# Four more low parts of two pooling groups by adding transfers, and each pooling group's newest columns ahead of later low parts on GpSimd

## The chip, the cores and the metric

One core of one Trainium2 chip runs the whole kernel in one launch. The metric is the device time of an execution in microseconds (us); the time before is the median of three runs.

## The reference

One layer of a hybrid decoder on 256 prompt columns and 8 x 4 sample columns, T = 288 columns in all, with 2048 channels, in float32:

```
h = rmsnorm(x, norm1_g)
proj = h @ w_in + b_in                       # 3072 columns: a, gate, z
u = a * sigmoid(gate)                        # 1024 channels
c = silu(layernorm(depthwise_causal_conv(concat(history, u), conv_w, conv_b)))   # 31 taps
d = multiscale_pool(concat(history, z))      # 4 groups, windows 2, 4, 8, 16
p = (d per group @ pool_w) * pool_scale
x = x + concat(c, p) @ w_out
x = x + square(relu(rmsnorm(x, norm2_g) @ w_ff1)) @ w_ff2
y = rmsnorm(x, norm_f)
```

The new convolution and pooling states are outputs too.

## The kernel before, in words

Channels lie on the 128 partitions and the 288 columns along the free side, so each matrix product is a sum of 128x128 weight tiles times 128x288 activations. Every product is done in three passes on rounded numbers: an activation or weight is split in a high part (`hi`, rounded to fp32r) and a low part (`lo` = raw - hi), and the sum takes hi x hi, lo x hi and hi x lo. Two k-tiles of one output tile make a group of six matmuls in `gemm`: two with weights `whi`, two with `wlo`, two with `whi`.

Weights come from `io["w"]` in blocks of 2048 or 1024 rows x 256 columns; a half of such a block (4 k-tiles, 512 KB) is loaded in one transfer by SP into a raw tile `wr` (6 buffers) and split into `whi` and `wlo` (5 buffers each). PE uses such a half part for 24 matmuls. The number behind a name (wlo14) counts the half parts in the order of use: wlo1 to wlo8 belong to the first two convolution pairs, wlo9 to wlo12 to `c2`, 13 to 16 to `c3`, 17 to 20 to `c4`, 21 to 24 to pooling group `p3`, 25 to 28 to `c5`, 29 to 32 to `p2`, 33 to the small product `P3`, 34 to 37 to `c6`, 38 to 41 to `p1`, 42 to `P2`, 43 to 46 to `p0`, 47 to `P1`, 48 to 51 to `c7`, 52 to `P0`, and from 53 on to the output projection (`w0`, `w1`, ...), then to the MLP.

`split_part` makes the high part on ACT always (line L260). The low part is made in one of three ways, chosen by the letter in the table `WAYS` for the stage and the place in it:
- `V`: one subtraction on DVE (L265);
- `G`: two subtractions of half the tile on GpSimd, called POOL in the profile (L268);
- `D`: ACT writes -hi into `lo` (L262) and a transfer issued by POOL adds the raw weights from memory onto it (L263).

The stages stand in `SEQUENCE`: c0 c1 c2 c3 c4 p3 c5 p2 P3 c6 p1 P2 p0 P1 c7 P0. A `c` stage (`conv_products`, `conv_pair`) makes two output tiles, the gated `u`, and then the convolution: the taps of the prompt columns on DVE (L448), those of the sample columns as one product `prd` on POOL (L451) and a sum on DVE. A `p` stage (`pool_group`) makes two tiles of `z`, running sums `s` by doubling on POOL (L479), and from them the pooled differences `d`: prompt columns on DVE (L484), the newest (sample) columns on POOL (L486, L487). A `P` stage (`pool_products`) multiplies `d` with the pooling weights. `gemm` takes its `between` as work put into its order ahead of a given k.

The order on each engine comes from a scheduler that places instructions by priority as the program is written, along a simulated timeline; `tc.issue_after(x)` puts an instruction behind x. On PE the order is held by a chain. Convolution taps are written under `later()`, with lower priority. The order of the matmuls inside a product can be altered: `classes` is a string that asks for matmuls of class 0 or 1 (parity of k plus the choice of the activation's part) in turn, and `TURN` is such a string, of 48 places, used in `c2`, `c5`, at the start of the output projection and in a few products after it. Everywhere else the six matmuls of a group follow each other as above. Product results go to two PSUM buffers `ac`, so a product must wait until the last but one is read.

Of the kernel before, what the change touches and what calls it, by code (L numbers as in the profile page):

```python
# [12 lines left out]
ALU = mybir.AluOpType  # L13
# [56 lines left out]
TURN = "110100" * 4 + "01" * 6 + "1100" * 3  # L70


WAYS = {"c2": "GVGV", "c3": "GDGG", "c4": "GDGD", "p3": "GDDG", "c5": "GDGD", "c": "GGGV", "p": "GVVG", "w0": "VV", "w": "GG", "ff": "VV"}


VEC = (("norm1_g", 16), ("b_in", 24), ("conv_b", 8), ("ln_g", 8), ("ln_b", 8), ("pool_scale", 8), ("norm2_g", 16), ("norm_f", 16))
# [10 lines left out]
def trunk_kernel(ctx: ExitStack, tc: tile.TileContext, io):  # L87
# [46 lines left out]
    def f32(t):  # L134
        return t.bitcast(F32)
# [25 lines left out]

    blocks = iter(range(5, io["w"].shape[0]))

    def load():

        src, raw = io["w"][next(blocks)], []
        for h in range(2):
            raw.append((raw_tile(), src[:, 4 * h : 4 * h + 4, :]))
            nc.sync.dma_start(*raw[-1])
        return raw  # L170
# [78 lines left out]
        last = mm(psum[:, 0, :T], minus, total, start=True, stop=True)  # L249
        return row_of(psum, psum[:, 0, :T], *args), last  # L250

    turns = {}

    def split_part(raw, src, hi, lo, way):

        nc.scalar.copy(hi, raw)  # L260
        if way == "D":
            nc.scalar.activation(lo, f32(hi), AF.Copy, scale=-1.0)  # L262
            nc.gpsimd.dma_start(lo, src, accum_op=ALU.add)  # L263
        elif way == "V":
            nc.vector.tensor_tensor(lo, raw, f32(hi), op=ALU.subtract)  # L265
        else:
            for j in range(0, raw.shape[1], 2):
                nc.gpsimd.tensor_tensor(lo[:, j : j + 2, :], raw[:, j : j + 2, :], f32(hi[:, j : j + 2, :]), op=ALU.subtract)  # L268

    def spl():  # L270
        return [wspl.tile([P, 4, 256], F32R, name=nm("w" + part), tag="w" + part) for part in ("hi", "lo")]
# [21 lines left out]
            chain[0] = last.ins  # L293
        return last

    def gemm(banks, rhs, m_outer=False, between={}, classes="", by_part=False, gets=None, pairs=None):


        n = len(rhs)
        gets = gets or ready.pop(0)  # L300
        todo, begins = [], {}
        if by_part:
            for k in range(0, n, 2):
                sets = [range(len(banks))] if k else [range(2), range(2, len(banks))]
# [24 lines left out]
        return last.ins
# [48 lines left out]
    def weight_groups():  # L378

        yield [lambda k, m, h=h: [t[:, m // 2, k % 2, m % 2 * P : (m % 2 + 1) * P] for t in firsts[4 * h + k // 2]] for h in range(2)]  # L380
        for kind, i in SEQUENCE[2:]:
            yield [pool_weights(i)] if kind == "P" else [split(load(), f"{kind}{i}") for _ in range(2)]
        for j in range(8):
            get = split(load(), f"w{j}")
            yield [lambda k, m, get=get: get(korder[k], m)]
        for _ in range(8):
            yield [split(load())]
        for _ in range(2 * DFF // 256):
            yield [split(load()) for _ in range(2)]
# [22 lines left out]
    rb = row("rb")  # L412


    cs, pcs = [], []
    sum_c = tmpp.tile([P, 2, T], F32, name="sum_c", tag="ag2", bufs=2)

    def history(i):
# [8 lines left out]
    def conv_pair(i, banks):  # L427
# [8 lines left out]
            nc.vector.scalar_tensor_tensor(out=out, in0=a, scalar=v("b_in", i), in1=b, op0=ALU.add, op1=ALU.mult)  # L436
        if i % 2 == 0:
            cs.append(actp.tile([P, 2, T], F32, name=nm("c"), tag="c", bufs=4))
        c = cs[i // 2][:, i % 2, :]
        with later():  # L440
            if i % 2 == 0:
# [6 lines left out]
                nc.vector.scalar_tensor_tensor(out=dst, in0=up[:, w : w + SEQ], scalar=cwv[:, w : w + 1], in1=pc, op0=ALU.mult, op1=ALU.add)  # L448
            prd = prdp.tile([P, NB, NS, CW + 1], F32, name=nm("prd"), tag="prd")
            nc.scalar.activation(prd[:, :, :, CW], ones[:, 0 : NB * NS].rearrange("p (b t) -> p b t", t=NS), AF.Identity, bias=v("conv_b", i), scale=0.0)  # L450
            nc.gpsimd.tensor_tensor(prd[:, :, :, 0:CW], windows(us, CW), cwv[:, None, None, :].to_broadcast([P, NB, NS, CW]), op=ALU.mult)  # L451
# [12 lines left out]
    def pool_group(g):  # L464
# [19 lines left out]
        nc.vector.scalar_tensor_tensor(out=d[:, :, 0:SEQ], in0=s[:, :, PH:ZO], scalar=1.0 / w, in1=z[:, :, PH:ZO], op0=ALU.mult, op1=ALU.subtract)  # L484
        news = [x[:, :, ZO:ZL].rearrange("p m (b t) -> p m b t", t=ZS)[:, :, :, PH:] for x in (s, z)]
        nc.gpsimd.tensor_scalar(news[0], news[0], 1.0 / w, None, op0=ALU.mult)  # L486
        nc.gpsimd.tensor_tensor(d[:, :, SEQ:T].rearrange("p m (b t) -> p m b t", t=NS), news[0], news[1], op=ALU.subtract)  # L487
        dh, dl = act2("dx", tag="p", bufs=4)
        nc.scalar.copy(dh, d)
        nc.vector.tensor_tensor(dl, d, f32(dh), op=ALU.subtract)  # L490
# [34 lines left out]
    for kind, i in SEQUENCE[3:-1]:  # L525
        if (kind, i) == ("P", 1):
            continue
        if kind == "c":
            conv_pair(i, conv_products(i, classes=TURN if i == 5 else "", **(dict(gets=ahead(1), between={12: lambda: pool_products(1)}) if i == 7 else {})))
        elif kind == "p":  # L530
            pool_group(i)
        else:
            pool_products(i)
    proj = [halves(dd[k // 2])[k % 2] for k in korder]
    bks = [bank2() for _ in range(2)]
    both_gets = [ahead(1) for _ in range(2)]
    early = [(k, m) for k in (0, 2, 4) for m in range(4)]
    early.sort(key=lambda km: km[1] // 2)
    gemm(each(bks[0]) + each(bks[1]), proj, gets=[lambda k, m: both_gets[m // 2][0](k, m % 2)], between={(0, 2): lambda: pool_products(0)}, classes="." * 36 + TURN, pairs=early + [(6, m) for m in range(4)])
    chain.clear()  # L540
    load_table(AF.Abs_reciprocal_sqrt, f32(mixp[1][0])[:, 0:1])
    with later(2 * LATER):
# [53 lines left out]
    chain.append(last)  # L596
    bks = [bank2() for _ in range(2)]
    two_gets = [ahead(0) for _ in range(2)]
    gemm(each(bks[0]) + each(bks[1]), mixc, gets=[lambda k, m: two_gets[m // 2][0](k, m % 2)])
    chain.clear()  # L600
    for g in range(8):
        bk = bks[g] if g < 2 else bank2()
# [179 lines left out]
```

## Time and profile before

| what | us |
|---|---|
| median of the runs (1081.53 to 1083.24) | 1081.72 |
| the profiled execution, its own time | 1082.43 |
| its span in the profile | 1080.6 |
| PE matmul busy | 1069.2 |
| DVE busy | 633.7 |
| ACT busy | 479.0 |
| POOL busy | 175.9 |

The page of the profile counts an engine as busy while an instruction of its own runs; PE's matmuls overlap, so that its busy time says little about how fast they follow each other. The span runs from the first to the last instruction; the execution's own time is 1.83 us longer. DVE and POOL are busiest in the first 210 us, where convolution, pooling and low parts share them; after that the MLP's weights are split by ACT and DVE alone.

### The profile page before, as it was taken

How to read it: one execution, taken by the hardware profiler on the slowest of the kernel's cores; microseconds unless marked ns; L12 is line 12 of the kernel's file. 1: busy time of each engine (PE TensorE's matmuls, PEld its weight loads, DVE VectorE, ACT ScalarE, POOL GpSimd, SP SyncE). 2: the span in 40 equal slices, each digit the busy share in tenths (PEclk: the TensorE clock that was granted, in tenths of full speed). 3: DMA queues.
4: the chain of work that ended last, by engine and by line, in shares of the span. 5: the costliest groups of instructions: out<-in, count | busy, mean ns of one | idle time of the engine just before them, and what ended most of it. 6: DMA issues, size and time to landing. Idle time of an engine off the chain costs nothing.

```text
span 1080.6 us, 19528 instructions
## 1 busy us (share of the span) xinstructions
PE 1069.2 (99%) x8176; PEld 1067.9 (99%) x8176; DVE 633.7 (59%) x810; ACT 479.0 (44%) x588; POOL 175.9 (16%) x182
## 2 busy tenths in 40 slices
PE   9999999999999999999999999999999999999996
PEld 8999999999999999999999999999999999999996
DVE  7899999788654544444554444555544445554553
ACT  8654445665544433334443333444433334444441
POOL 0878979512000000000000000000000000000001
PEclk9999999999999999999999999999999999999999
DMA  9896478555555555555555555555555555555522
GB/s 326 288 263 182 145 187 247 177 171 173 162 173 166 169 175 163 170 173 165 170 174 164 170 170 167 171 173 162 173 168 167 173 171 164 173 166 170 172 79 88
DMA packets 58296, 190.71 MB, mean 176 GB/s; under 512 B 6240, under 2 KB 11232, under 8 KB 58208
## 3 DMA queue, kind: packets, MB, share of 16 engines
q1 hardware_dynamic: 56336, 184.35, 54.3%
q0 software_dynamic: 1008, 3.67, 1.9%
q8 instruction: 64, 1.05, 0.4%
q10 hardware_dynamic: 864, 1.44, 0.4%
q14 instruction: 24, 0.20, 0.0%
HBM read 185.16 MB, written 4.28 MB: 175 GB/s over the span
## 4 chain that ended last, share of the span: by engine, by line
PE 75%; issue 21%; ACT 2%; POOL 1%; DMA 1%; SPq 0%; POOLq 0%; DVE 0%
PE ac L291 74%; POOL wlo L268 1%; DMA wr<-in_w 1%; ACT whi L349 1%; PE pp L291 1%; DMA wlo<-in_w 1%; ACT hx L354 0%; ACT z_all L405 0%; POOL prd L451 0%; POOL xT L718 0%; ACT whi L260 0%; SPq L191 0%; POOLq L768 0%; DVE xT L691 0%; ACT whi L356 0%
## 5 line engine op out<-in xcount | busy, mean ns | idle before, releaser
L260 ACT CAST whi<-wr 128x1024 fp32r<-128x1024 f32 (+1 forms) x332 | 346.5, 1044 | 551.3 <-PE ac L291 536.7
L265 DVE TENSOR_TENSOR wlo<-wr,whi 128x1024 fp32r<-128x1024 f32 x288 | 353.5, 1227 | 348.1 <-ACT whi L260 348.1
L291 PE MATMUL ac<-ax,whi 128*128 128x288 f32 x2048 | 351.0, 292 | 0.0
L291 PE MATMUL ac<-fx,whi 128*128 128x288 f32 x2048 | 350.2, 292 | 0.0
L291 PEld LDWEIGHTS ac<-ax,whi 128*128 128x128 f32 x2048 | 296.0, 187 | 0.0
L291 PEld LDWEIGHTS ac<-fx,whi 128*128 128x128 f32 x2048 | 295.6, 187 | 0.0
L291 PE MATMUL ac<-ax,wlo 128*128 128x288 f32 x1024 | 217.3, 292 | 0.0
L291 PE MATMUL ac<-fx,wlo 128*128 128x288 f32 x1024 | 216.4, 292 | 0.0
L291 PEld LDWEIGHTS ac<-ax,wlo 128*128 128x128 f32 x1024 | 162.5, 187 | 0.0
L291 PEld LDWEIGHTS ac<-fx,wlo 128*128 128x128 f32 x1024 | 162.2, 187 | 0.0
L291 PE MATMUL ac<-hx,whi 128*128 128x288 f32 x768 | 131.9, 296 | 1.4 <-DVE hx L352 1.4
L718 POOL TENSOR_TENSOR xT<-xT,rf 128x288 f32<-128x288 f32 x4 | 3.1, 795 | 799.9 <-ACT rf L722 799.9
L291 PEld LDWEIGHTS ac<-hx,whi 128*128 128x128 f32 x768 | 112.6, 190 | 1.8 <-ACT hx L354 1.7
L268 POOL TENSOR_TENSOR wlo<-wr,whi 128x512 fp32r<-128x512 f32 x74 | 102.4, 1433 | 17.1 <-ACT whi L260 16.0
L448 DVE SCALAR_TENSOR_TENSOR pc<-u_all,vec,pc 128x256 f32<-128x256 f32 x232 | 99.3, 479 | 1.9 <-ACT pc L445 0.7
L291 PE MATMUL ac<-hx,wlo 128*128 128x288 f32 x384 | 80.4, 295 | 0.2 <-DMA wlo<-in_w 0.2
L291 PEld LDWEIGHTS ac<-hx,wlo 128*128 128x128 f32 x384 | 61.1, 189 | 0.4 <-DMA wlo<-in_w 0.4
L291 PE MATMUL ac<-dx,whi 128*128 128x288 f32 x256 | 46.8, 295 | 0.0
L291 PE MATMUL ac<-mx,whi 128*128 128x288 f32 x256 | 44.9, 293 | 0.0
L660 DVE SCALAR_TENSOR_TENSOR t<-ac,r 128x576 f32<-128x576 f32 x32 | 24.2, 757 | 25.4 <-PE ac L291 25.3
L291 PEld LDWEIGHTS ac<-dx,whi 128*128 128x128 f32 x256 | 38.4, 188 | 0.2
L291 PEld LDWEIGHTS ac<-mx,whi 128*128 128x128 f32 x256 | 37.5, 188 | 0.2 <-DVE xT L579 0.2
(129 smaller groups left out, 529.6 us busy)
## 6 DMA issues: line engine op xcount, KB each, us to landing
wr<-in_w SPq DMA_DIRECT2D x335, 512.0 KB, 3.8
wlo<-in_w POOLq DMA_DIRECT2D x7, 512.0 KB, 7.8
xT<-in_xT SPq DMA_DIRECT2D x8, 288.0 KB, 7.7
wr<-in_w SPq DMA_DIRECT2D x5, 256.0 KB, 3.9
out_u_out<-u_all SPq DMA_DIRECT2D x1, 1208.0 KB, 9.6
u_all<-in_hist_c SPq DMA_DIRECT2D x8, 136.0 KB, 5.3
out_z_out<-z_all SPq DMA_DIRECT2D x1, 668.0 KB, 9.2
z_all<-in_hist_p SPq DMA_DIRECT2D x4, 152.0 KB, 6.6
```

Of the source, the lines that this page charges most:

```text
L260: nc.scalar.copy(hi, raw)
L265: nc.vector.tensor_tensor(lo, raw, f32(hi), op=ALU.subtract)
L268: nc.gpsimd.tensor_tensor(lo[:, j : j + 2, :], raw[:, j : j + 2, :], f32(hi[:, j : j + 2, :]), op=ALU.subtract)
L291: last = nc.tensor.matmul(*args, **kw)
L349: nc.scalar.copy(hi[:, blocks[0]], raw[:, blocks[0]])
L448: nc.vector.scalar_tensor_tensor(out=dst, in0=up[:, w : w + SEQ], scalar=cwv[:, w : w + 1], in1=pc, op0=ALU.mult, op1=ALU.add)
L660: nc.vector.scalar_tensor_tensor(out=t, in0=bk[:, :, :T], scalar=0.0, in1=both(rows2[0]), op0=ALU.max, op1=ALU.mult)
L718: eng.tensor_tensor(xk, xk, r[:, None, :].to_broadcast([P, n, T]), op=ALU.mult)
```

## The change

Seven edits, of which the first, the third and the fourth name most of what moves:
1. `WAYS`: both inner parts of `p2` and of `p1` (wlo30, 31, 39, 40) go from `V` to `D`; the second part of `c4` (wlo18) goes from `D` to `G`; the first part of the output projection (wlo53) goes from `V` to `G`. `D` has ten parts where it had seven.
2. The two halves of every weight block of the output projection's pooled rows are loaded, split and numbered in the other order, so that the half that PE uses first is made first.
3. In `pool_group` the newest columns of `d` (POOL) are written ahead of the prompt columns (DVE), and low parts made on POOL are put behind the last pooling group's newest columns.
4. Each `prd` is put behind an adding transfer (i up to 4) or behind a pooling group's newest columns (5, 6, 7).
5. The convolutions of pairs 2 and 3 are written one pair later.
6. The product `P1` moves from ahead of the last quarter of `c7` to ahead of its second half; `P0` moves into the output projection 12 matmuls earlier; the first 24 matmuls of that projection take all `whi` first, then `wlo`.
7. In the first two products of the convolution's half of the output projection, the first buffer `ac22` takes four k-tiles (24 matmuls) before `ac23` begins, where it took two (12).

```diff
-WAYS = {"c2": "GVGV", "c3": "GDGG", "c4": "GDGD", "p3": "GDDG", "c5": "GDGD", "c": "GGGV", "p": "GVVG", "w0": "VV", "w": "GG", "ff": "VV"}
+WAYS = {"c2": "GVGV", "c3": "GDGG", "c4": "GGGD", "c5": "GDGD", "c": "GGGV", "p3": "GDDG", "p0": "GVVG", "p": "GDDG", "w0": "GV", "w": "GG", "ff": "VV"}
...
-    def load():
+    def load(order=(0, 1)):
...
-        for h in range(2):
+        for h in order:
...
-    turns = {}
+    turns, added, newest, pooled = {}, [], {}, []
...
-            nc.gpsimd.dma_start(lo, src, accum_op=ALU.add)
+            added.append(nc.gpsimd.dma_start(lo, src, accum_op=ALU.add))
...
-                nc.gpsimd.tensor_tensor(lo[:, j : j + 2, :], raw[:, j : j + 2, :], f32(hi[:, j : j + 2, :]), op=ALU.subtract)
+                with tc.issue_after(pooled[-1].ins) if pooled else nullcontext():
+                    nc.gpsimd.tensor_tensor(lo[:, j : j + 2, :], raw[:, j : j + 2, :], f32(hi[:, j : j + 2, :]), op=ALU.subtract)
...
+        todo[:late] = sorted(todo[:late], key=lambda p: p[2])
...
-            get = split(load(), f"w{j}")
-            yield [lambda k, m, get=get: get(korder[k], m)]
+            get = split(load((1, 0)), f"w{j}")
+            yield [lambda k, m, get=get: get(korder[k] ^ 4, m)]
...
+        while waiting:
+            taps(*waiting.pop())
+        if i in (2, 3):
+            waiting.append((i, up, us))
+        else:
+            taps(i, up, us)
...
+            with tc.issue_after((newest[{5: 3, 6: 2, 7: 0}[i]] if i > 4 else added[max(0, min(2, i - 1))]).ins):
+                nc.gpsimd.tensor_tensor(prd[:, :, :, 0:CW], windows(us, CW), cwv[:, None, None, :].to_broadcast([P, NB, NS, CW]), op=ALU.mult)
...
-        nc.vector.scalar_tensor_tensor(out=d[:, :, 0:SEQ], in0=s[:, :, PH:ZO], scalar=1.0 / w, in1=z[:, :, PH:ZO], op0=ALU.mult, op1=ALU.subtract)
         nc.gpsimd.tensor_scalar(news[0], news[0], 1.0 / w, None, op0=ALU.mult)
-        nc.gpsimd.tensor_tensor(d[:, :, SEQ:T].rearrange("p m (b t) -> p m b t", t=NS), news[0], news[1], op=ALU.subtract)
+        last = nc.gpsimd.tensor_tensor(d[:, :, SEQ:T].rearrange("p m (b t) -> p m b t", t=NS), news[0], news[1], op=ALU.subtract)
+        newest[g] = last
+        nc.vector.scalar_tensor_tensor(out=d[:, :, 0:SEQ], in0=s[:, :, PH:ZO], scalar=1.0 / w, in1=z[:, :, PH:ZO], op0=ALU.mult, op1=ALU.subtract)
...
-... between={12: lambda: pool_products(1)}
+... between={8: lambda: pool_products(1)}
...
-... between={(0, 2): lambda: pool_products(0)}, classes="." * 36 + TURN
+... late=24, between={4: lambda: pool_products(0)}, classes="." * 24 + TURN
...
-    gemm(each(bks[0]) + each(bks[1]), mixc, gets=[lambda k, m: two_gets[m // 2][0](k, m % 2)])
+    gemm(each(bks[0]) + each(bks[1]), mixc, gets=[lambda k, m: two_gets[m // 2][0](k, m % 2)], pairs=mixed)
```

What this does to the order. On POOL, around the first adding transfer (wlo14, in `c3`), before; `prd1` and `prd2` are the sample convolutions of the first two pairs:

```order
L268 TENSOR_TENSOR wlo13_604<-wr13_599,whi13_603 128x512 x2
L451 TENSOR_TENSOR prd1_667<-u_all_87,vec_85 128x32x31
L451 TENSOR_TENSOR prd2_708<-u_all_87,vec_85 128x32x31
L263 DMA wlo14_609<-in_w 128x1024
L268 TENSOR_TENSOR wlo15_618<-wr15_613,whi15_617 128x512 x2
```

The same place on POOL after the change:

```order
L269 TENSOR_TENSOR wlo13_604<-wr13_599,whi13_603 128x512 x2
L263 DMA wlo14_609<-in_w 128x1024
L463 TENSOR_TENSOR prd1_667<-u_all_87,vec_85 128x32x31
L463 TENSOR_TENSOR prd2_708<-u_all_87,vec_85 128x32x31
L269 TENSOR_TENSOR wlo15_618<-wr15_613,whi15_617 128x512 x2
```

The transfer's issue now stands ahead of the two convolutions. In the same way `prd4` now stands between the issues of wlo22 and wlo23 in `p3`, where it stood ahead of both.

On POOL in `p1` (low parts 38 to 41), before; `s5` to `s7` are the running sums of group 1, `sum_c` a sum of convolutions:

```order
L268 TENSOR_TENSOR wlo36_1571<-wr36_1566,whi36_1570 128x512 x2
L479 TENSOR_TENSOR s5_1522<-z_all_91 128x422 x2
L479 TENSOR_TENSOR s6_1525<-s5_1522 128x420
L268 TENSOR_TENSOR wlo38_1686<-wr38_1681,whi38_1685 128x512 x2
L479 TENSOR_TENSOR s6_1525<-s5_1522 128x420
L456 TENSOR_TENSOR sum_c_251<-c1_634,c2_718 128x288
L479 TENSOR_TENSOR s7_1528<-s6_1525 128x416 x2
L268 TENSOR_TENSOR wlo41_1703<-wr41_1696,whi41_1702 128x512 x2
```

The same place on POOL after the change:

```order
L269 TENSOR_TENSOR wlo36_1573<-wr36_1568,whi36_1572 128x512 x2
L269 TENSOR_TENSOR wlo38_1688<-wr38_1683,whi38_1687 128x512 x2
L491 TENSOR_TENSOR s5_1524<-z_all_91 128x422 x2
L468 TENSOR_TENSOR sum_c_251<-c1_634,c2_718 128x288
L263 DMA wlo39_1693<-in_w 128x1024
L491 TENSOR_TENSOR s6_1527<-s5_1524 128x420 x2
L263 DMA wlo40_1702<-in_w 128x1024
L269 TENSOR_TENSOR wlo41_1707<-wr41_1699,whi41_1706 128x512 x2
```

The issues of the two adding transfers stand between the running sums, and wlo38 ahead of all of them. In `p2` the order is alike: the issue of wlo30 stands behind the first half of `s2`, that of wlo31 behind the second half, and both ahead of `s3`.

On PE, at the start of the convolution's half of the output projection, before (`mx1`, `mx2` are its first k-tiles, two in each):

```order
L291 MATMUL ac22_2841<-mx1_2816,wlo69_2742 128x288 x2
L291 MATMUL ac22_2841<-mx1_2816,whi69_2741 128x288 x2
L291 MATMUL ac23_2842<-mx1_2816,whi71_2803 128x288 x2
L291 MATMUL ac23_2842<-mx1_2816,wlo71_2804 128x288 x2
L291 MATMUL ac23_2842<-mx1_2816,whi71_2803 128x288 x4
```

The same place on PE after the change:

```order
L292 MATMUL ac22_2846<-mx1_2821,wlo69_2747 128x288 x2
L292 MATMUL ac22_2846<-mx1_2821,whi69_2746 128x288 x2
L292 MATMUL ac22_2846<-mx2_2828,whi69_2746 128x288 x2
L292 MATMUL ac22_2846<-mx2_2828,wlo69_2747 128x288 x2
L292 MATMUL ac22_2846<-mx2_2828,whi69_2746 128x288 x4
```

`ac23` now begins 12 matmuls later, behind the whole of wlo69's half part.

More of the change, by code (lines that the diff above doesn't have):

```diff
@@ L294, in mm, with gemm @@
         return last
-    def gemm(banks, rhs, m_outer=False, between={}, classes="", by_part=False, gets=None, pairs=None):
+    def gemm(banks, rhs, m_outer=False, between={}, classes="", by_part=False, gets=None, pairs=None, late=0):
         n = len(rhs)
@@ L412, in trunk_kernel @@
     rb = row("rb")
-    cs, pcs = [], []
+    cs, pcs, waiting = [], [], []
     sum_c = tmpp.tile([P, 2, T], F32, name="sum_c", tag="ag2", bufs=2)
@@ L450, in conv_pair @@
             nc.scalar.activation(prd[:, :, :, CW], ones[:, 0 : NB * NS].rearrange("p (b t) -> p b t", t=NS), AF.Identity, bias=v("conv_b", i), scale=0.0)
-            nc.gpsimd.tensor_tensor(prd[:, :, :, 0:CW], windows(us, CW), cwv[:, None, None, :].to_broadcast([P, NB, NS, CW]), op=ALU.mult)
+            with tc.issue_after((newest[{5: 3, 6: 2, 7: 0}[i]] if i > 4 else added[max(0, min(2, i - 1))]).ins):
+                nc.gpsimd.tensor_tensor(prd[:, :, :, 0:CW], windows(us, CW), cwv[:, None, None, :].to_broadcast([P, NB, NS, CW]), op=ALU.mult)
             cso = c[:, SEQ:T]
@@ L527, in trunk_kernel @@
             continue
+        if i == 7:
+            pooled.append(newest[1])
         if kind == "c":
-            conv_pair(i, conv_products(i, classes=TURN if i == 5 else "", **(dict(gets=ahead(1), between={12: lambda: pool_products(1)}) if i == 7 else {})))
+            conv_pair(i, conv_products(i, classes=TURN if i == 5 else "", **(dict(gets=ahead(1), between={8: lambda: pool_products(1)}) if i == 7 else {})))
         elif kind == "p":
@@ L532, in trunk_kernel @@
         else:
+            pooled.append(newest[i])
             pool_products(i)
+    pooled.append(newest[0])
     proj = [halves(dd[k // 2])[k % 2] for k in korder]
@@ L538, in trunk_kernel @@
     early.sort(key=lambda km: km[1] // 2)
-    gemm(each(bks[0]) + each(bks[1]), proj, gets=[lambda k, m: both_gets[m // 2][0](k, m % 2)], between={(0, 2): lambda: pool_products(0)}, classes="." * 36 + TURN, pairs=early + [(6, m) for m in range(4)])
+    mixed = [(k, m) for k in range(0, KT // 2, 2) for m in range(4)]
+    mixed.sort(key=lambda km: (km[0] // 4, km[1] // 2) if km[0] < 4 else (1, 0))
+    gemm(each(bks[0]) + each(bks[1]), proj, gets=[lambda k, m: both_gets[m // 2][0](k, m % 2)], late=24, between={4: lambda: pool_products(0)}, classes="." * 24 + TURN, pairs=early + [(6, m) for m in range(4)])
     chain.clear()
```

1 line of the change is left out of this document (added).

## The prediction

> **What bounds the kernel now.** I read the page first, then PE's waits, then the matmuls counted in windows, then PE's timeline at the places where the count falls short.
>
> ```profile
> span 1080.6 us, 19528 instructions
> PE 1069.2 (99%) x8176; PEld 1067.9 (99%) x8176; DVE 633.7 (59%) x810; ACT 479.0 (44%) x588; POOL 175.9 (16%) x182
> ```
>
> ```profile
> 22.00:31.00 9.00, 9.00 (x71) 1.00 0.97 333
> 54.00:84.00 30.00, 30.00 (x228) 1.00 0.97 258
> 100.00:160.00 60.00, 60.00 (x464) 1.00 0.56 165
> 220.00:231.00 11.00, 11.00 (x85) 1.00 0.56 175
> ```
>
> PE is busy all the time, so every other engine matters only through what PE waits for, or how fast its matmuls follow each other. In the windows (stretch; PE busy and matmuls; granted clock; DMA share; GB/s) the clock is 1.00 everywhere, and yet the rate differs. Each window counts some two matmuls that reach over its edges: 60 us hold 462, 129.9 ns each, while 30 us from 54 hold 226, 132.7 ns, and 11 us from 220 hold 83, 132.5 ns. DMA load is not it: 22 to 31 and 54 to 84 have the same share, 0.97, and the first has 69 in 9 us (130.4), and 220 to 231 is slow at 0.56. What the two slow stretches have in common stands in PE's timeline (start, duration, count):
>
> ```profile
> 48.77 0.68 PE L291 MATMUL ac<-hx,whi 128*128 128x288 f32 x4
> 49.55 0.68 PE L291 MATMUL ac<-hx,whi 128*128 128x288 f32 x4
> 50.42 0.54 PE L291 MATMUL ac<-hx,wlo 128*128 128x288 f32 x2 [0.20 <-DMA wlo<-in_w]
> 50.80 0.69 PE L291 MATMUL ac<-hx,whi 128*128 128x288 f32 x4
> 51.32 0.43 PE L291 MATMUL ac<-hx,wlo 128*128 128x288 f32 x2
> 52.12 0.43 PE L291 MATMUL ac<-hx,wlo 128*128 128x288 f32 x2
> ...
> 218.93 0.42 PE L291 MATMUL ac<-mx,wlo 128*128 128x288 f32 x2
> 219.19 0.90 PE L291 MATMUL ac<-mx,whi 128*128 128x288 f32 x4
> 219.93 0.43 PE L291 MATMUL ac<-mx,wlo 128*128 128x288 f32 x2
> ```
>
> Ahead of 50.42 six matmuls take 0.78 us (48.77 to 49.55). Then PE waits for wlo14, an adding transfer: the pair should have come at 49.55 + 0.52 = 50.07. Behind the wait six take 0.80 (51.32 to 52.12). At 219.19 four matmuls take 0.74 until the next instead of 0.52. So PE, once it has been stopped, runs 0.02 us per six, 3.33 ns per matmul, slower, and both stretches end where the program has a `TURN` (`c5`; the product behind the two first ones of the convolution's half). I read this as one mechanism: a stop puts PE in a slower step, a `TURN` brings it out.
>
> **The change part by part.** *wlo14's issue ahead of prd1 and prd2* (POOL's timeline; times from issue to landing of the seven adding transfers):
>
> ```profile
> 40.16 4.33 POOL L451 TENSOR_TENSOR prd<-u_all,vec 128x992 f32<-128x992 f32 x2
> 44.41 1.01 POOL L263 DMA_DIRECT2D wlo<-in_w  x1
> ...
> DMA to landing us min/median/max: 6.0/7.8/10.2
> ```
>
> It can be issued some 4 us earlier, at 40.2 to 40.5, and lands at 46.2 to 50.7 by the shortest and the longest of the seven; it took 6.0 itself, and fewer transfers are in flight now. So it is there by 50.07. Gain: 50.42 - 50.07 = 0.35 for the wait, 0.12 for the slow pair behind it (50.80 - 50.42 = 0.38 instead of 0.26), and the slower step until `c5`: of `c3` 22 + 2 x 24 matmuls are left, `c4` and `p3` have 96 each, 262 x 3.33 ns = 0.87. Together 1.34 us. The step's share lies between 0 (it has another cause) and 0.87; I take 0.87, because the step changes at the wait and, 170 us later, at the other one.
>
> *ac22 with 24 matmuls.* At 219.19 PE waits for `ac23`'s buffer, which DVE reads last here:
>
> ```profile
> 218.75 0.74 DVE L579 TENSOR_TENSOR xT<-xT,ac 128x576 f32<-128x576 f32 x1
> ```
>
> It ends at 219.49; PE now wants the buffer 12 matmuls, 1.56 us, after 219.45, and does not wait. Gain: 0.22, and of this product's 96 matmuls 84 at 3.33 ns, 0.28, together 0.50. In exchange `mx2` is wanted 1.6 us earlier; the DVE instruction ahead of the quoted one makes its last piece, so that it is ready.
>
> *The issues in p3.* `prd4` now stands between the issues of wlo22 and wlo23:
>
> ```profile
> 65.99 0.88 POOL L263 DMA_DIRECT2D wlo<-in_w  x1
> DMA to landing us min/median/max: 9.8/9.8/9.8
> 68.90 0.87 POOL L263 DMA_DIRECT2D wlo<-in_w  x1 [2.04 <-ACT wlo L262]
> 79.32 0.43 PE L291 MATMUL ac<-hx,wlo 128*128 128x288 f32 x2
> ```
>
> `prd4`'s 2.2 us fit into the 2.04 that POOL waited there, so 0.2 is lost; wlo23 landed at 68.90 + 10.2 = 79.1, 0.2 before use, and the quicker step takes 4 x 24 x 3.33 ns = 0.32 off its time. Against that wlo18, now made on POOL, is out of the line of transfers that delays wlo20, 22 and 23. It costs between 0 and 0.6 (0.3 of waiting, 0.12, and 48 slow matmuls to `c5`, 0.16). I take 0: half a megabyte less to add is worth more than 0.3 where the shortest transfer takes 6.0 and these two take 10.
>
> *Four adding transfers in p2 and p1.* Off DVE they go; nobody waits for DVE there. Each needs a -hi on ACT (1.06) and an issue on POOL (0.9), and must land before PE's first `wlo`:
>
> ```profile
> 88.82 1.06 ACT L260 CAST whi<-wr 128x1024 fp32r<-128x1024 f32 x1 [0.88 <-PE ac L291]
> L262 ACT ACTIVATE wlo<-whi 128x1024 fp32r<-128x1024 f32 x7 | 7.4, 1059 | 0.2
> ...
> 92.03 6.55 POOL L479 TENSOR_TENSOR s<-s 128x420 f32<-128x420 f32 x6
> L479 POOL TENSOR_TENSOR s<-s 128x420 f32<-128x420 f32 x6 | 6.7, 1134 | 0.0
> ...
> 101.40 0.42 PE L291 MATMUL ac<-hx,wlo 128*128 128x288 f32 x2
> 104.52 0.42 PE L291 MATMUL ac<-hx,wlo 128*128 128x288 f32 x2
> ```
>
> For wlo30 ACT is ready at 88.82 + 2 x 1.06 = 90.9; POOL issues behind `s2`'s first half, at 92.03 + 1.13 = 93.2. PE wants it at 101.40: 8.2 us. wlo31 goes out at 93.2 + 0.9 + 1.1 = 95.2 and is wanted at 104.52. Two that follow closely land 3.3 us apart (65.99 + 9.8 = 75.8, then 79.1). In p1:
>
> ```profile
> 78.74 0.88 POOL L263 DMA_DIRECT2D wlo<-in_w  x1
> DMA to landing us min/median/max: 6.3/6.3/6.3
> ...
> 102.56 0.39 POOL L486 TENSOR_SCALAR s<-s 128x64 f32<-128x64 f32 x1 [0.81 <-DVE d L484]
> 113.50 2.71 POOL L479 TENSOR_TENSOR s<-z_all 128x422 f32<-128x422 f32 x2
> 117.02 3.53 POOL L268 TENSOR_TENSOR wlo<-wr,whi 128x512 fp32r<-128x512 f32 x2
> 122.41 0.80 POOL L456 TENSOR_TENSOR sum_c<-c,c 128x288 f32<-128x288 f32 x1
> ...
> 127.92 0.42 PE L291 MATMUL ac<-hx,wlo 128*128 128x288 f32 x2
> 131.04 0.42 PE L291 MATMUL ac<-hx,wlo 128*128 128x288 f32 x2
> ```
>
> POOL reaches wlo38 at 117.02 + 1.8 (two issues) - 0.81 (the wait for DVE is gone) - 3.52 (the sums from 113.50 stand behind it) = 114.5. Then 2.5 to 3.5, `s5` 2.71, `sum_c` 0.80: wlo39 goes out at 120.5 to 121.5, wanted at 127.92, which leaves 6.4 to 7.4. wlo40 lands 3.3 behind wlo39, at 129.8 to 131.1 if that takes 6.0 or 6.3, wanted at 131.04. With another adding transfer in flight ahead, 8 to 10 are seen; alone, 6.0 and 6.3. wlo30 and wlo39 are alone and plain loads are at half the DMA share (0.56 in the window from 100), so I take 6.3: nothing waits, with 1.9, 1.7, 0.1 to 1.1 and about 0 to 1.2 to spare. Cost 0; with 10.2 for the first of each pair it is 7.3 (below). The Trainium skill, page "DMA: Bandwidth & Descriptors", section "Anatomy of one DMA — SWDGE (gpsimd) path", gives a fixed 2.0 us and bytes over 436 GB/s, an estimate of 3.2 us for these 512 KB; by it none of the four could be late and the sum would stand. The trace's shortest is 6.0, so I don't follow it.
>
> *The rest at nothing.*
>
> ```profile
> L268 POOL TENSOR_TENSOR wlo<-wr,whi 128x512 fp32r<-128x512 f32 x74 | 102.4, 1433 | 17.1 <-ACT whi L260 16.0
> POOL s L486 <- DVE d L484: 6.8, 4, 4.5
> 171.34 0.29 PE L291 MATMUL ac<-dx,whi 128*128 128x288 f32 x1
> ```
>
> wlo18 and wlo53 put 2 x 2 x 1.43 = 5.7 us on POOL, the newest columns ahead of DVE take 6.8 of its waiting away. `P1` and `P0` earlier rest on that too: their `d` no longer stands behind low parts or the 4.5 us wait; if it were late, PE would stop ahead of 171. The halves' new order in the output projection gives each low part 3 us more or less, in PE's favour.
>
> Sum: -1.34 - 0.50 = -1.84 us. On the profiled execution's 1082.43 that is 1080.6; the median stands 0.71 lower, so 1079.9.
>
> **The rivals.** (1) *The slower step has nothing to do with the stop.* Then only 0.35 + 0.12 + 0.22 go: 1081.0. For it: no row says what the step is. Against: it starts in the very pair that waited, twice. [...]
>
> (2) *A new wait in p2 or p1.* wlo31 or wlo40 misses by a few tenths. Then PE runs in the slower step up to the next `TURN`, in the output projection's first product, about 171.34: from 131.04 310 matmuls, 1.03 us; from 101.40 538, 1.79. With 0.3 of waiting and 0.12: 1.45 to 2.2 back, 1081.3 to 1082.1. For it: wlo40's margin is about nothing. The Trainium skill's DMA page, section "SWDGE vs HWDGE vs iDMA", says that only one queue is allocated for transfers issued by GpSimd, so the second of a pair stands behind the first; the 3.3 us between two landings agree.
>
> (3) *Slower: the first of each pair lands as late as wlo23 did.* wlo30 at 93.2 + 10.2 = 103.4, 2.0 late; wlo39 at 121 + 10.2 = 131.2, 3.3 late; with 1.79 and 0.24 that is 7.3, net +5.5, 1087.2. It ends above the old time by 0.2% (2.16 us) once both take over 8.6 us. Against: what took that long stood behind another adding transfer.
>
> **How the numbers follow.** The forecast as summed 0.45, (1) 0.13, (2) 0.33, (3) 0.07, a wait elsewhere of either size 0.02. The forecast's own spread is about 0.5 us, from the p3 term and from the three runs (two within 0.2, one 1.5 above). 0.2%, 2.16 us, is about what a measurement of this kernel can tell from no change; that is below 1079.56, which a fifth of the forecast's cases reach: faster 0.10. Slower, (3) and a little of (2): 0.08. Same: 0.82. The range 1079.4 to 1082.3 holds the forecast, (1) and (2), and leaves out (3) and the tails.
>
> **What would show it.** After the change PE's waits should have no row for wlo; 54 to 84 should hold 233 matmuls instead of 228 and 220 to 231 87 instead of 85; the ten landings should include four of 6 to 9 us. A wait row for wlo, or 132.7 ns per matmul in 100 to 160, is rival (2); 228 in 54 to 84 without a wait is rival (1). The forecast is wrong if adding transfers in quiet DMA time take over 8 us, or if another engine's wait shows on PE.

## The result, and the profile after

The changed kernel takes 1085.33 us (median of 14 runs, 1083.54 to 1086.50) against 1081.64 for the kernel before: ratio 1.0031, 95% interval 1.0023 to 1.0038. It is slower, by 3.7 us; 1079.9 was predicted, with a range to 1082.3. The profiled execution took 1084.51 (before 1082.43). From its page:

```profile
span 1082.7 us, 19544 instructions
PE 1068.7 (99%) x8176; PEld 1066.9 (99%) x8176; DVE 634.6 (59%) x805; ACT 481.8 (45%) x591; POOL 182.1 (17%) x189
...
wlo<-in_w POOLq DMA_DIRECT2D x10, 512.0 KB, 9.4
```

Ten adding transfers instead of seven, and the median from issue to landing went from 7.8 to 9.4 us. PE's waits have a row that was forecast not to be there (total, times, longest):

```profile
PE ac L292 <- DMA wlo<-in_w: 1.4, 1, 1.4
```

The windows that answer to those of before (for 100 to 160 a piece on either side of the stop). Behind the stretch and its length stand the busy time and the instructions of PE, of PE's weight loads, of DVE, ACT and GpSimd, then the granted clock, the DMA share and GB/s:

```profile
54.00:84.00 30.00, 30.00 (x233) 30.00 (x232) 28.62 (x69) 17.77 (x22) 25.85 (x20) 1.00 0.92 253
100.00:127.00 27.00, 27.00 (x205) 26.98 (x203) 26.58 (x52) 14.33 (x20) 25.80 (x24) 1.00 0.62 183
143.00:167.00 24.00, 24.00 (x182) 24.00 (x181) 24.00 (x49) 12.00 (x19) 22.45 (x22) 1.00 0.69 160
220.00:231.00 11.00, 11.00 (x87) 11.00 (x86) 7.37 (x9) 5.78 (x9) 0.00 (x0) 1.00 0.55 167
```

The first and the last hold 233 and 87 matmuls, as forecast: both gains are there. The two between, less the two at their edges, give 27.00 / 203 = 133.0 and 24.00 / 180 = 133.3 ns per matmul where 129.9 stood before: PE is in its slower step from 100 us on. PE's timeline shows where it begins and where it stops (the last two rows are the mean of the convolutions and the end):

```profile
100.16 0.48 PE L292 MATMUL ac<-hx,wlo 128*128 128x288 f32 x2
...
126.86 0.70 PE L292 MATMUL ac<-hx,whi 128*128 128x288 f32 x4
128.98 0.53 PE L292 MATMUL ac<-hx,wlo 128*128 128x288 f32 x2 [1.43 <-DMA wlo<-in_w]
...
200.18 0.65 PE L292 MATMUL pmean<-sum_c,ones 128*128 128x288 f32 x2
...
1070.92 1.14 PE L721 MATMUL idle<-ones 128*128 128x128 f32 x8
```

The last two in the kernel before:

```profile
197.96 0.65 PE L291 MATMUL pmean<-sum_c,ones 128*128 128x288 f32 x2
...
1069.18 1.14 PE L702 MATMUL idle<-ones 128*128 128x128 f32 x8
```

This is a balance. At wlo30 PE is 101.40 - 100.16 = 1.24 us ahead of before. At wlo39 it is 128.98 - 127.92 = 1.06 behind: it stood from 126.86 + 0.53 to 128.98, 1.59, and the slower step took the other 0.7 (some 205 matmuls x 3.33 ns). At 200 us it is 2.22 behind, 1.16 more: 0.11 for the pair behind the stop and 322 slow matmuls, 1.07. At the end 1.74: the edit of `ac22` gave 0.48. The last stores take 0.36 more, together the 2.1 us between the two spans. So 1.7 us of gain came in, and about 3.5 went to wlo30, 0.06 us late, and wlo39. These are two single executions, 2.1 us apart, where the medians are 3.7 apart: the one before lies 0.8 above its median, the one after 0.8 below.

### The profile page after: what moved, and what is told of

It reads as the page before. It is cut to its first block, busy times and chain, and to the rows that moved or that the text cites. A ratio compares the mean times of both kernels' runs of the same rounds, so it can differ in the third digit from the quotient of the medians.

```text
span 1082.7 us, 19544 instructions
## 1 busy us (share of the span) xinstructions
PE 1068.7 (99%) x8176; PEld 1066.9 (99%) x8176; DVE 634.6 (59%) x805; ACT 481.8 (45%) x591; POOL 182.1 (17%) x189
## 3 DMA queue, kind: packets, MB, share of 16 engines
q8 instruction: 64, 1.05, 0.4%
## 4 chain that ended last, share of the span: by engine, by line
PE 74%; issue 20%; DVE 2%; DMA 2%; ACT 1%; POOL 0%; SPq 0%; POOLq 0%; DVEq 0%; ACTq 0%
PE ac L292 74%; DMA wlo<-in_w 1%; DVE pc L459 1%; DMA wr<-in_w 1%; PE pp L292 0%; DVE wlo L265 0%; POOL xT L737 0%; DVE dx L503 0%; ACT hx L356 0%; ACT whi L351 0%; DVE z_all L409 0%; ACT z_all L407 0%; DVE wlo L360 0%; DVE c L465 0%; ACT wlo L262 0%
## 5 line engine op out<-in xcount | busy, mean ns | idle before, releaser
L269 POOL TENSOR_TENSOR wlo<-wr,whi 128x512 fp32r<-128x512 f32 x78 | 107.3, 1445 | 17.6 <-ACT whi L260 16.3
```

## The experiments

Two theories on why the transfers were late stood at the start. A: plain loads take the DMA engines first, and `D` itself sends more of them ahead, since the raw tile is free once ACT has made the high part. B: the two adding transfers of a group slow each other. C was the rival to both: the loss lies in other edits. What speaks for A is the share of the 16 DMA engines by queue around wlo39, issued at 119.60 (q1 the plain loads, q0 the adding transfers; first 120 to 124, then 124 to 129):

```profile
q1 hardware_dynamic: 298, 1.10, 89.0%
q0 software_dynamic: 1, 0.00, 0.8%
...
q0 software_dynamic: 223, 0.85, 86.0%
q1 hardware_dynamic: 95, 0.31, 19.1%
```

For 4 us behind its issue the transfer moved one packet. SP's issues of the four loads in question, after, and then the same four before (start, and the stretch they cover):

```profile
115.98 4.26 SPq L169 DMA_DIRECT2D wr<-in_w  x4
```

```profile
114.64 7.41 SPq L169 DMA_DIRECT2D wr<-in_w  x4
```

Before, they went out over 7.4 us; now over 4.3. The second, at 117.88, and the last, at 119.91, go out as soon as ACT has read `wr39` and `wr40`, the raw tiles of the two `D` parts.

**dve_again.** The four low parts back on DVE in the changed kernel.

```diff
-"p": "GDDG"
+"p": "GVVG"
```

> The changed kernel with wlo30, 31, 39 and 40 back on DVE, the other edits kept. Theory A (the loss is all from adding transfers in p2 and p1 that land 9.3 to 9.5 us after issue: 1.7 us of stop at wlo39 and some 1.8 us of slower step from wlo30 to the output projection) and theory B (the same, but late because the two of a group slow each other): 1079.8 to 1080.8, 0.1% below the kernel before, no wait for wlo and 130.0 ns per matmul from 100 to 160 us. Rival C (the loss is from the other edits, GpSimd's new order or the start): it stays above 1083.5.

Measured: 1085.78 (1084.97 to 1086.04), ratio 1.0033 (1.0021 to 1.0046). A and B as written were both wrong: without the four transfers the kernel is as slow. C's time came, above 1083.5, by a wait that none of the three had named. No row for wlo is left, and PE waits for DVE:

```profile
PE pp L292 <- DVE dx L515: 1.8, 1, 1.8
```

On DVE's and PE's timelines (`pp` is P0's product, L515 reads the product of P1 ahead of it, L503 makes the low part of `d`):

```profile
163.07 0.51 DVE L515 SCALAR_TENSOR_TENSOR dx<-pp,vec,dx 128x288 fp32r<-128x288 f32 x1
165.80 1.45 DVE L503 TENSOR_TENSOR dx<-d,dx 128x576 fp32r<-128x576 f32 x1
167.56 0.51 DVE L515 SCALAR_TENSOR_TENSOR dx<-pp,vec,dx 128x288 fp32r<-128x288 f32 x1
...
168.12 0.53 PE L292 MATMUL pp<-dx,whi 128*128 128x288 f32 x2 [1.76 <-DVE dx L515]
```

The kernel before at the same place, and then, by windows, DVE's busy time (the number behind PEld's):

```profile
167.24 0.50 DVE L502 SCALAR_TENSOR_TENSOR dx<-pp,vec,dx 128x288 fp32r<-128x288 f32 x1
...
169.78 0.42 PE L291 MATMUL pp<-dx,whi 128*128 128x288 f32 x2
```

```profile
140.00:160.00 20.00, 20.00 (x156) 20.00 (x155) 20.00 (x42) 9.84 (x17) 17.24 (x18) 1.00 0.69 184
160.00:170.00 10.00, 10.00 (x79) 10.00 (x78) 10.00 (x22) 5.95 (x8) 7.03 (x7) 1.00 0.86 255
```

DVE was busy 20.00 of 20 us there before the change too, and its last read for P1 ended 169.78 - 167.74 = 2.0 us ahead of PE's use. PE would now come there 1.56 earlier by the edit of P0's place and 2.0 more in this execution, of which 1.3 stand at 38 us already, ahead of the first edited place. DVE does not come earlier: its last read ends at 168.07.

**held_loads.** Behind the issue of the four transfers one column of the raw tile is read by GpSimd, so that the tile is loaded anew only then.

```diff
-"p": "GDDG"
+"p": "GHHG"
...
+        def hold():
+            with tc.issue_after(added[-1].ins):
+                nc.gpsimd.tensor_scalar(held, raw[:, 3, 255:256], 1.0, None, op0=ALU.mult)
...
-            added.append(nc.gpsimd.dma_start(lo, src, accum_op=ALU.add))
+            added.append(nc.gpsimd.dma_start(lo, src, accum_op=ALU.add)); way == "H" and hold()
```

> The changed kernel, with one more GpSimd instruction of one column behind each of the four issues in p2 and p1 that reads the raw tile, so that the tile, which ACT has finished with, isn't loaded anew before the adding transfer is issued. Theory A (each transfer begins only when the plain loads issued just ahead of it are through, and the earlier release of the raw tiles put two loads more ahead of it): wlo30 and wlo39 land 6.3 to 8 us after issue instead of 9.3 to 9.4, no stop over 0.3 us in 100 to 135, 1080 to 1082. Theory B (the two of a pair slow each other): 9 us and more as before, a stop of 1.5 to 2 us for wlo39, 1084.5 to 1086.5.

Measured: 1085.98, ratio 1.0035 (1.0022 to 1.0048), no gain; but the landings of wlo30 and of wlo39, and the queues' shares at wlo39 in 121 to 124 and in 124 to 127:

```profile
DMA to landing us min/median/max: 5.6/5.6/5.6
...
DMA to landing us min/median/max: 8.9/8.9/8.9
```

```profile
q0 software_dynamic: 86, 0.35, 65.5%
q1 hardware_dynamic: 38, 0.11, 8.8%
...
q1 hardware_dynamic: 106, 0.43, 56.1%
q0 software_dynamic: 55, 0.16, 29.1%
```

wlo30 took 5.6 instead of 9.4 with its pair partner still behind it and one load fewer ahead of it. That speaks for the loads, but not for 3.8 us of them: with the loads at the same places as in the changed kernel wlo30 took 6.7 in three_added and 6.9 in four_alone, below. wlo39's first packet moved 1.6 us behind its issue instead of 4.3, and then it was overtaken by the load that the held tile let go at 121.33. So A holds with an addition: a load delays the transfer when it goes out ahead of it and also when it goes out in the middle of it. The Trainium skill, page "DMA: Bandwidth & Descriptors", section "Issuing engines are not separate DMA queues", says that transfers of all issuing engines run on the same 16 DMA engines and interleave; the trace agrees, with 29.1% left for q0 beside 56.1%.

**first_of_pair.** Only wlo30 and wlo39 by adding transfers.

```diff
-"p": "GDDG"
+"p": "GDVG"
```

> The changed kernel with only the first of each pair (wlo30, wlo39) by an adding transfer; wlo31 and wlo40 on DVE. Theory B (pair): alone in its queue the transfer lands 6.0 to 7 us after issue, no stop, 1080 to 1081. Theory A (loads ahead): the raw tile of the one part is still released early, wlo31's and wlo40's are not, so one load fewer stands ahead: 7.5 to 9 us, wlo39 up to 1 us late, 1081 to 1084.

Measured: 1083.22 (1082.34 to 1084.97), ratio 1.0011 (1.0002 to 1.0020). Landings:

```profile
wlo<-in_w POOLq DMA_DIRECT2D x1, 512.0 KB, 7.8
...
wlo<-in_w POOLq DMA_DIRECT2D x1, 512.0 KB, 9.2
```

Alone in its queue, wlo39 still takes 9.2 us: B falls. The prediction had laid the 10.2 us of wlo23 to a transfer ahead of it; that was this same wrong reason. The first packet of wlo39 moved 2.1 us behind its issue at 120.05, and the queues show where the rest went (122 to 126, then 126 to 129):

```profile
q0 software_dynamic: 121, 0.47, 67.4%
...
q1 hardware_dynamic: 237, 0.65, 60.6%
q0 software_dynamic: 23, 0.05, 9.1%
```

0.47 of its 0.52 MB were through at 126, and the last 23 packets took three more us beside plain loads. The profiled execution (1084.86) stopped 1.2 us for wlo39 and 0.8 in `p3`; it is among the slowest of the eleven.

**p2_only.** The two of `p2` by transfers, the two of `p1` on DVE.

```diff
-"p": "GDDG"
+"p2": "GDDG", "p": "GVVG"
```

> The changed kernel with the adding transfers of p2 kept and those of p1 (wlo39, wlo40) back on DVE. If a stop of any length starts the slower step (133.3 ns per matmul instead of 130.0) until the next TURN: wlo30 some 0.06 us late, no other stop, 133.3 ns from 100 to 172 us, 1.8 us more than with all four on DVE, 1081.6 to 1082.6. If the slower step needs the long stop: 130.0 ns, and the time of the kernel with all four on DVE.

Measured: 1086.18, ratio 1.0035 (1.0023 to 1.0048). wlo30 came 0.58 us in time in its profiled execution, so the question asked was not put. The other case was: without a stop at wlo30, 100 to 127 us holds 210 matmuls, 27.00 / 208 = 129.8 ns, where the changed kernel, stopped for 0.06 us there, had 133.0. PE waited 1.9 us for DVE instead (`u_all`, L438, at 172). Two low parts off DVE are not enough.

**two_gains.** The kernel before with the two edits that the prediction credits, and no other.

```diff
-            nc.gpsimd.tensor_tensor(prd[:, :, :, 0:CW], ...)
+            with tc.issue_after(added[0].ins) if i < 2 else nullcontext():
+                nc.gpsimd.tensor_tensor(prd[:, :, :, 0:CW], ...)
...
-    gemm(each(bks[0]) + each(bks[1]), mixc, gets=...)
+    gemm(each(bks[0]) + each(bks[1]), mixc, gets=..., pairs=mixed)
```

> The kernel before with only two of the edits: prd1 and prd2 behind the issue of wlo14, and four k-tiles of ac22 ahead of ac23. The prediction's sum (-1.34 and -0.50 us, the slower step ends with the stops) holds by itself: 1.84 us below the kernel before, ratio 0.9983, no wait of PE behind 40 us for wlo or ac23. Rival (DVE's slack at P0, 2.1 us before, is used up by a PE that comes earlier): a stop ahead of P0 at about 168 with slower matmuls behind it, ratio 0.999 to 1.002.

Measured: 1085.74 (1083.21 to 1089.48), ratio 1.0038 (1.0026 to 1.0050). The rival's stops came, and cost more than it said. The stop for wlo14 is gone, and in its place PE stops three times:

```profile
159.93 0.54 PE L291 MATMUL pp<-dx,whi 128*128 128x288 f32 x2 [0.32 <-ACT dx L490]
161.26 0.79 PE L291 MATMUL pp<-dx,whi 128*128 128x288 f32 x4 [0.54 <-DVE dx L491]
170.38 0.80 PE L291 MATMUL ac<-dx,whi 128*128 128x288 f32 x4 [0.88 <-DVE dx L503]
```

PE was only 1.0 us earlier there, less than the 2.0 that DVE had in hand. DVE itself was late: its last read for P1 ended at 170.32 instead of 167.74. Its own instructions took longer, as the four low parts of `d` up to 171 us show, before and then here (count; busy time, mean ns):

```profile
L490 DVE TENSOR_TENSOR dx<-d,dx 128x576 fp32r<-128x576 f32 x4 | 4.3, 1068 | 0.0
```

```profile
L491 DVE TENSOR_TENSOR dx<-d,dx 128x576 fp32r<-128x576 f32 x4 | 6.5, 1623 | 0.0
```

With `d` (3.4 to 3.8) and the low parts of the weights (17.2 to 18.3) that is 3.7 us. At least one of them met GpSimd's work: the low part of `d` for group 2 beside `prd`, and the same instruction in the kernel before (second fence; the sums `s5` to `s7` that lead to it, three doublings, are those of group 2, not of group 1):

```profile
129.82 2.58 DVE L491 TENSOR_TENSOR dx<-d,dx 128x576 fp32r<-128x576 f32 x1
...
129.59 2.19 POOL L452 TENSOR_TENSOR prd<-u_all,vec 128x992 f32<-128x992 f32 x1 [1.24 <-DVE u_all L436]
```

```profile
131.44 0.99 DVE L490 TENSOR_TENSOR dx<-d,dx 128x576 fp32r<-128x576 f32 x1
```

The Trainium skill, page "SBUF — State Buffer", section "SBUF: two separate sides", says that a VectorE instruction with two SBUF inputs and a GpSimd instruction that reads SBUF share a port pair, and that the later one waits for the whole of the other. 2.58 us beside a `prd` of 2.19 against 0.99 fits; for the other instructions it was not shown.

**old_places.** dve_again with P1 and P0 at their old places.

```diff
-between={8: lambda: pool_products(1)}
+between={12: lambda: pool_products(1)}
-late=24, between={4: lambda: pool_products(0)}, classes="." * 24 + TURN
+between={(0, 2): lambda: pool_products(0)}, classes="." * 36 + TURN
```

> dve_again (four low parts back on DVE) with P1 and P0 at the places they had before the change. DVE is late there because P0 comes 12 matmuls, 1.56 us, earlier and PE 2 us earlier, against 2.1 us of slack before: with the old places the stop of 2.05 us ahead of P0 shrinks to 0 to 0.5 us, the clock stays at 1.00 behind it, 1081 to 1083. Rival (the convolutions written one pair later make DVE late, wherever P0 stands): a stop of 1.5 us and more in 160 to 185 remains, 1084 to 1086.

Measured: 1086.29, ratio 1.0038 (1.0025 to 1.0052). The rival's stops came: 1.4 and 0.8 us, for `dx` of P1's result (ACT L514 and DVE L515), at 169 and 171, and a granted clock of 0.72 behind them (172 to 176). The place of P0 is not what makes DVE late. The rival's reason, the later convolutions, is not shown by this: two_gains has such stops without them.

**four_alone.** The four transfers alone in the kernel before.

```diff
-"p": "GVVG"
+"p0": "GVVG", "p": "GDDG"
```

> The kernel before with only the four low parts wlo30, 31, 39, 40 by adding transfers. If plain loads that the earlier release of raw tiles pulls ahead make them late in any order: wlo30 and wlo39 take 8 to 10 us from issue to landing, wlo39 goes out some 4 us later than in the changed kernel and stops PE for 4 us and more, with a low clock behind the stop, 1087 to 1091. By the prediction's 6.3 us the stop would be 0 to 3 us.

Measured: 1094.27 in one execution. wlo39 took 9.0 us, as expected, and wlo30 6.9, less than expected; but the stop came elsewhere:

```profile
117.49 0.85 PE L291 MATMUL pp<-dx,whi 128*128 128x288 f32 x2 [7.88 <-ACT dx L489]
```

In the old order the newest columns of group 3 stand behind low parts on GpSimd; with the issues among them they are done at 116.7 instead of 105.9, and P3 finds its `dx` 7.9 us late. In the changed kernel, which puts the newest columns first, PE has no such stop.

**turn_in_c4.** `TURN` in `c4` too, in the kernel before.

```diff
-classes=TURN if i == 5 else ""
+classes=TURN if i in (4, 5) else ""
```

> The kernel before with TURN in c4 too. The prediction's reading (a stop puts PE in a slower step, a TURN brings it out): the stop for wlo14 at 50 us stays, 133.3 ns per matmul from there to c4's start at about 57, and 130.0 through the rest of c4 and p3 instead of 133.3; some 0.5 us less. Rival (the step of 54 to 84 has to do with the products or the loads there): 133.3 ns until c5 as before.

Measured: 1080.69 in one execution. From 64 to 77 us, this kernel and then the kernel before:

```profile
64.00:77.00 13.00, 13.00 (x102) 13.00 (x101) 12.29 (x29) 7.75 (x10) 9.45 (x9) 1.00 0.98 266
```

```profile
64.00:77.00 13.00, 13.00 (x100) 13.00 (x99) 12.05 (x29) 8.00 (x11) 9.22 (x8) 1.00 1.01 266
```

13.00 / 100 = 130.0 ns instead of 13.00 / 98 = 132.7, with the stop at 49 us still there. The slower step follows a stop and ends at a `TURN`. The time of the execution says less: it was 1.4 us ahead of the kernel before's at 38 us already, and `TURN` added 0.4.

**two_gains_less_dve, dve_again_less_dve, before_less_dve.** Ten taps of the convolution left out, 4.1 us of DVE's work, in two_gains, in dve_again and in the kernel before.

```diff
-            for w in range(1, CW):
+            for w in range(6 if i in (4, 5) else 1, CW):
```

> two_gains with five taps each (the 2nd to the 6th) left out of the convolutions of pairs 4 and 5: 10 instructions, some 4.1 us, less on DVE ahead of P1 and P0. If DVE is what takes the two gains back (its dx for P1 and P0 and the read of their results come late once PE is 1.3 us earlier): no stop of PE from 140 to 180, clock 1.00, 1079.5 to 1080.5, the 1.84 us that the prediction summed. Rival (the stops have another cause than DVE's load): stops at 159, 161 and 169 stay, 1083 to 1087.

> dve_again (the changed kernel with the four low parts on DVE) with the same ten taps left out. If the changed kernel loses by the late transfers with the four D's, and by DVE's lateness without them: neither is there now, no stop from 100 to 200 over 0.3 us, 1079.5 to 1080.8, the predicted time. Rival (another of its edits costs by itself): 1083 and more.

> The kernel before with the same ten taps left out of the convolutions of pairs 4 and 5, as a control. DVE is not waited for by PE there, so the kernel keeps its time within 0.4 us: 1081.2 to 1082.0. Rival (the taps cost time by themselves): 1080 or less, and what the two kernels with fewer taps gained is theirs.

Measured: two_gains falls from 1085.74 to 1082.87 (ratio 1.0017, 1.0007 to 1.0027), dve_again from 1085.78 to 1081.43 (0.9996, 0.9987 to 1.0004), and the control stays at 1081.62 (1.0000, 0.9990 to 1.0009). DVE's load is what PE waited for in the two. 4.1 us are not enough for either to reach the 1079.9 of the prediction: one wait for DVE is left in the first (wlo54, 1.3 us at 164), and stops of under 0.4 in the second.

**turn_c4_and_mixed.** The kernel before with the edit of turn_in_c4 and that of `ac22` (`pairs=mixed`, as in two_gains).

> The kernel before with TURN in c4 and four k-tiles of ac22 ahead of ac23. PE comes only 0.6 us earlier at P1 and P0, less than the 2.1 us that DVE has there, and the second gain lies behind both: no new stop, 0.6 + 0.5 = 1.1 us less than before, ratio 0.9990, and 130.0 ns in c4, p3 and from 220 on. Rival (any earlier PE finds DVE late): a stop in 155 to 172 and 1082 to 1085.

Measured: 1080.88 (1080.12 to 1081.98) against 1081.80, ratio 0.9993 (0.9984 to 1.0002). The trace has what was expected, with no new stop (220 to 231 holds 87 matmuls instead of 85):

```profile
220.00:231.00 11.00, 11.00 (x87) 11.00 (x86) 6.74 (x9) 5.90 (x10) 0.61 (x1) 1.00 0.46 144
```

P0 comes at 168.50 instead of 169.78 and DVE's last read for P1 ends at 166.46 instead of 167.74: where the order on GpSimd and DVE is left alone, DVE keeps its 2.0 us in hand. Of the kernels that leave nothing out and ran more than once it is the fastest, 0.9 us below the kernel before, though its interval just takes in no change.

**after_second_look.** The changed kernel again, with no edit.

> The changed kernel once more. Its 14 times fall in two groups, 1083.5 to 1085.0 and 1085.7 to 1086.5. If the upper group is a low granted clock behind a stop of over about 2 us for wlo39: with a time of 1085.5 or more the stop at 127 us is over 1.9 us long and the granted clock is below 0.7 in the 4 us behind it; with a time below 1085.0 the stop is shorter and the clock is 1.00. Rival: the groups differ elsewhere (the start, or p3).

Measured: 1085.33, between the two groups, with the clock at 1.00. It had the longer stop and not the low clock. The rest lies in p3, where nothing waited in the first profile (PE's timeline, then its waits):

```profile
75.16 0.53 PE L292 MATMUL ac<-hx,wlo 128*128 128x288 f32 x2 [0.19 <-DMA wlo<-in_w]
78.94 0.53 PE L292 MATMUL ac<-hx,wlo 128*128 128x288 f32 x2 [0.32 <-DMA wlo<-in_w]
```

```profile
PE ac L292 <- DMA wlo<-in_w: 2.5, 3, 2.0
```

wlo22 and wlo23 are late here, and wlo39 by 2.0 instead of 1.4. How late a transfer lands differs from execution to execution, and with it the time. Whether that explains all of the upper group of times is open.

**turns_behind_stop.** The changed kernel with `TURN` in `c6` and `p0` too.

```diff
-classes=TURN if i == 5 else ""
+classes=TURN if i in (5, 6) else ""
...
-        gemm(each(bk), hx)
+        gemm(each(bk), hx, classes=TURN if g == 0 else "")
```

> The changed kernel with TURN in c6 and p0 too; GpSimd, DVE and ACT keep their order. If the slower step belongs to the stop and ends at a TURN: 133.3 ns from 100 to 111, 130.0 in c6 and p1 until wlo39, whose stop gets 0.4 us longer (what c6 gains is waited for there), 133.3 until p0, 130.0 from p0 (140) to the output projection: some 240 matmuls x 3.33 ns = 0.8 us less than the changed kernel, ratio 1.0024 to the kernel before. Rival (the slower step is the loads' or DVE's doing): 133.3 ns throughout, the time unchanged.

Measured: 1084.26, ratio 1.0024 (1.0015 to 1.0034), as expected. From 143 to 167 us:

```profile
143.00:167.00 24.00, 24.00 (x186) 24.00 (x185) 24.00 (x48) 12.15 (x19) 22.43 (x22) 1.00 0.67 168
```

24.00 / 184 = 130.4 instead of 133.3 ns. Only `p0`'s `TURN` was tested by this: wlo30 came in time here, 100 to 110 holds 79 matmuls (129.9 ns), and `c6` had no slower step to end. The stop for wlo39 grew from 1.59 to 2.1, as what PE gains ahead of it is waited for.

**three_added.** turns_behind_stop with wlo39 on DVE.

```diff
-"p": "GDDG"
+"p2": "GDDG", "p": "GVDG"
```

> turns_behind_stop with wlo39 back on DVE; wlo30, 31 and 40 stay adding transfers. wlo40 goes out at 120 to 121.5 and is wanted at 129.5: with 8 to 9.5 us it is 0 to 1.5 us late, or in time, instead of wlo39's 1.9 to 2.3. DVE has one low part more (1.2 us) than in the changed kernel. If a place between the two limits is left: no stop over 0.5 us in 100 to 185, 1079.5 to 1081. If one of them still binds: a stop of 0.5 to 1.5 us for wlo40, or for DVE's dx at 160 to 172, 1081 to 1084.

Measured: 1085.79, ratio 1.0035 (1.0021 to 1.0049). wlo40 was 0.06 us late, wlo22 and wlo23 again 0.5 each, and with one low part more DVE is late again:

```profile
174.24 0.37 PE L292 MATMUL ac<-dx,whi 128*128 128x288 f32 x1 [1.84 <-DVE u_all L438]
```

No way of dividing the four that was tried fits between the two limits.

## Why the prediction was wrong

- **wlo14's issue ahead of prd1 and prd2: right.** It landed 7.3 us after its issue, PE did not stop, and the step is 130.0 ns until `c5`; 1.24 of the 1.34 us stood at 100 us.
- **ac22 with 24 matmuls: right**, 0.48 for 0.50.
- **The issues in p3: mis-sized.** 0 was taken, with 0.6 as the bound. The changed kernel's first profile had no wait; the second had two, which cost 0.35 and 0.48 between starts beyond a step of 130 ns, 1.05 with the slow pairs behind them. Of the ten profiled executions with this order of p3 three lost nothing there, and seven lost 0.15 to 1.26 us.
- **Four adding transfers in p2 and p1, at 6.3 us for the first of each pair: the step that failed.** They took 9.4, 9.4, 9.3 and 9.5, and wlo39 stopped PE for 1.59 us. Between the ends 6.3 and 10.2 the choice was by whether another adding transfer was in flight; first_of_pair showed that not to be the cause, and the kernel before had shown it: the transfer issued at 54.86, with none ahead of it, took 7.8 us, and the one at 84.97, whose forerunner landed at 85.09, took 6.9. What stood ahead of wlo39 was plain loads, and the mean DMA share of 0.56 in 100 to 160 hid that four of them stand together there. Two of the four stand there because `D` frees the raw tile early; with one of these (first_of_pair) or both (held_loads) taken away the first packet moved 2.2 to 2.7 us sooner, and other loads, in the middle of the transfer, took that back. What a transfer takes with no load beside it no run shows.
- **The times at which PE wants the four: the sum's own gain was left out.** They are those of the kernel before, and the sum brings PE there 1.34 us earlier. Of the four margins 1.9, 1.7, 0.1 to 1.1 and 0 to 1.2 only the first two stay above nothing, so that by its own 6.3 us wlo39 would have been up to 1.2 us late. It was luck that this slip did not count: wlo39 was issued at 119.60 for 120.5 to 121.5, and with 6.3 us it would have been there 0.8 us ahead of PE.
- **The page's estimate.** The estimate of 3.2 us by the Trainium skill, page "DMA: Bandwidth & Descriptors", section "Anatomy of one DMA — SWDGE (gpsimd) path", which the prediction set aside, was further off.
- **The text's own rivals.** Rival (3) had the late landing of the first of each pair with a wrong reason, at 0.07; rival (2) had the slower step until 171, 1.79 us, and 0.7 + 1.07 of it was lost, beside the stop of 1.59. "Wrong if adding transfers in quiet DMA time take over 8 us" was the right test.
- **"Nobody waits for DVE there": true of the kernel before, and no price for what the other edits do to DVE.** DVE had 2.0 us in hand at P0. An earlier PE alone does not use that up (turn_c4_and_mixed); with the order on GpSimd changed DVE's own instructions took longer as well, 3.7 us in two_gains, where the sum's -1.84 became +4. In the changed kernel the four transfers pay for this, by relieving DVE, whose last read for P1 ends 3.7 us ahead of P0, and are late themselves.

## What to carry to other kernels

Before work is moved on one engine, read how much the next one has in hand in each stage behind it: DVE's 59% of the whole span was 20.00 of 20 us where it counted, so that each instruction that took longer there made it late. A transfer that replaces an engine's work also frees its buffers earlier; the loads that this starts are the ones it will queue behind. The mean DMA share of a long window says nothing of the 4 us behind an issue: count the loads there. A margin is taken against the time at which the changed kernel will want the data.

## What the runs showed of the hardware

- A stop, even one of 0.06 us, leaves PE at 133.3 instead of 130.0 ns per matmul for as long as groups of six in the plain order follow: 43 us in the changed kernel. The alternating order `TURN` ends it (turn_in_c4, turns_behind_stop). What in PE does this no row says.
- Some stops of about 2 us were followed by a low granted clock. Behind the 1.9 us stop of dve_again and the 2.3 us stop of held_loads the granted clock was 0.60 and 0.57 (windows of the two, in that order):

```profile
168.00:172.00 4.00, 3.88 (x18) 3.88 (x19) 3.96 (x12) 1.64 (x3) 4.00 (x4) 0.60 0.98 374
```

```profile
129.00:133.00 4.00, 3.90 (x18) 3.90 (x19) 3.93 (x11) 2.10 (x3) 1.35 (x4) 0.57 0.95 290
```

13 or 14 matmuls of 240 ns, 1.4 to 1.5 us lost. Behind after_second_look's stop of 2.2 us and three_added's of 2.0 the clock was 1.00, so length alone does not decide. The Trainium skill, page "TensorE: Matmul & The Clock Gate", section "What's actually happening", tells of a free-running activity window, which would fit stops of one length ending differently; its window of about 3.4 us is longer than the stops that lowered the clock here.
